# Six K pairs more by Strassen's products in a decoder block: two in the first feed-forward block pair, four in the down projection

## The chip, the cores and the metric

The kernel runs on one core of a Trainium2 chip. The metric is the device time of one execution in microseconds (us), median over three runs. The core's engines are TensorE (PE, matmuls), VectorE (DVE), ScalarE (ACT), GpSimd (POOL) and SyncE (SP, which issues most DMAs). Each works through its own queue of instructions; semaphores order them against each other.

## The reference

One decoder layer on x of 256 x 2048 in float32: an RMSNorm, a mixer block (one wide input projection, four branches, gates, output projection), a second RMSNorm, a SwiGLU feed-forward of width 5632, and a final RMSNorm. The change touches only the feed-forward:

```python
v = rms_norm(h, norm_ffn[l])
h = h + (jax.nn.silu(v @ w_ffn_gate[l]) * (v @ w_ffn_up[l])) @ w_ffn_down[l]
return rms_norm(h, norm_final)
```

## The kernel before

Every large product is made of float32 operands that are split in two: hi is the operand rounded to float32r (by ACT), lo the rest (by DVE), and a product is hi·hi + hi·lo + lo·hi, three matmuls of 128x128 by 128x512 (`mm3s`, lines 215 to 220).

`pair` (line 247) computes the product of the 256 rows with two neighbouring column blocks of 512, wl and wr, over `nkp` K pairs of 2 x 128 rows. Its results are the PSUM tiles q0 and q1 (one for each 128 rows of the output). A K pair is done in one of two ways. The plain one takes 8 products, 24 matmuls, and calls `wpiece` (line 118) for the two weights: a DMA `raw` on SP, `whi` on ACT, `wlo` on DVE; raw, whi and wlo have four buffers each. If the pair's number is in `skps` it is done by the Strassen (Winograd) form with 7 products, 21 matmuls: `s_weights` (line 222) loads the two weights into `sx`, makes four sums on DVE (`se`, `sx`), and splits the two tiles into `sh`/`sl` and `seh`/`sel` (ACT the first of each, DVE the second). sx, sh, sl, seh and sel have two buffers, se one. Four of the products go to PSUM tiles of their own, p1, p5, p6 and p7, which after the last Strassen pair are combined into u. The activations need sums too, `vsh`/`vsl`, for the pairs that are done in this form.

The feed-forward (lines 904 to 921) is 11 calls of `pair`, f = 0 to 10, each with 8 K pairs, gate and up columns as wl and wr. The normalized activations are vth/vtl, transposed by PE from hn: the closures in `later` do this for the last two quarters (12 transposes inside f=0, for pairs 4 to 7), and `run_later` is called at the third pair (`late["at"]` is 2) or, in a call with Strassen pairs that begin earlier, after the last one of them. ACT makes vth, DVE vtl. FS, the pairs whose activation sums are kept, is (0, 2, 3, 5). After each f, `nat_out` (line 318) transposes the hidden block hd and writes it to DRAM as hid (POOL's queue), also through `later`.

The down projection (lines 924 to 972) is two calls of `pair`, cc = 0 and 1, each with 22 K pairs; `h_of` loads hid back into a ring of three slots of `fin` (SP) and splits it into `ah` (ring of four). `split` holds the last pairs back so that q0 finishes first. DSS names the Strassen pairs of either half.

The order of each engine's instructions is made by the scheduler when the kernel is built; it follows the code's order but moves instructions forward where their inputs are ready by its own model.

Of the kernel before, what the change touches and what calls it, by code (L numbers as in the profile page):

```python
# [17 lines left out]
NKT = D // P  # L18
# [11 lines left out]
def hybrid_block_kernel(  # L30
# [13 lines left out]
    w_fg = w_ffn_gate[0]  # L44
    w_fu = w_ffn_up[0]
# [10 lines left out]
    def act(o, i, f=AF.Copy, **kw):  # L56
        return nc.scalar.activation(o, i, f, **kw)  # L57

    def tt(o, a, b, op, eng=None):
        return (eng or nc.vector).tensor_tensor(out=o, in0=a, in1=b, op=op)  # L60
# [9 lines left out]
    late = {"psum": None, "turn": 0, "at": 1}  # L70
# [144 lines left out]
    def mm3s(acc, a, w, first, last, pin=False):  # L215

        for x_, w_, st, sp_ in ((a[0], w[0], first, False), (a[0], w[1], False, False), (a[1], w[0], False, last)):
            m = nc.tensor.matmul(acc, x_, w_, start=st, stop=sp_)  # L218
            if pin:
                tc.keep_in_program_order(m)  # L220

    def s_weights(wl, wr, kp):
        sx, nb = late["sx"], late["sx_bufs"]
        rows = slice(kp * 2 * P, (kp + 1) * 2 * P)
        x_ = sx.tile([P, 4, 512], F32, tag="sx", name="sx", bufs=nb)
        nc.sync.dma_start(x_[:, 0:2, :], wr[rows, :].rearrange("(k p) n -> p k n", p=P))
        nc.sync.dma_start(x_[:, 2:4, :], wl[rows, :].rearrange("(k p) n -> p k n", p=P))
        e = sx.tile([P, 3, 512], F32, tag="se", name="se", bufs=1)
        h, lo = (sx.tile([P, 4, 512], F32R, tag=t, name=t, bufs=nb) for t in ("sh", "sl"))
        eh, el = (sx.tile([P, 3, 512], F32R, tag=t, name=t, bufs=nb) for t in ("seh", "sel"))  # L230
        tt(e[:, 0, :], x_[:, 0, :], x_[:, 1, :], ALU.add)
        tt(x_[:, 0, :], x_[:, 0, :], x_[:, 2, :], ALU.add)
        tt(e[:, 1, :], x_[:, 0, :], x_[:, 1, :], ALU.add)
        tt(e[:, 2, :], e[:, 1, :], x_[:, 3, :], ALU.add)
        act(h, x_)
        tt(lo, x_, rd(h), ALU.subtract)
        act(eh, e)
        tt(el, e, rd(eh), ALU.subtract)
        t1, r2, l1, l2 = ((h[:, i, :], lo[:, i, :]) for i in range(4))
        t3, t2, t4 = ((eh[:, i, :], el[:, i, :]) for i in range(3))  # L240
        return l1, l2, r2, t1, t2, t3, t4

    def run_later():
        while later:
            later.pop(0)()

    def pair(wl, wr, nkp, skps, a_of, upool=None, split=0, quiet=False, at_mid=None, order=None, own=False):

        pq = late["psum"]
        qt = [late["acc"].tile([P, 2, 512], F32, tag=f"q{t}", name=f"q{t}") for t in range(2)]
        q = [[qt[t][:, i, :] for i in range(2)] for t in range(2)]
        p = {}
        ns = len(skps)
        left = {(0, 0): 2 * nkp - ns, (0, 1): 2 * nkp - ns, (1, 0): 2 * nkp - ns, (1, 1): 2 * (nkp - ns),
                1: ns, 5: ns, 6: ns, 7: ns}
        begun = set()
        u = None
        if own:  # L260
            left[1, 0], left[1, 1] = left[1, 0] - 2 * split, left[1, 1] - 2 * split
            left[2, 0] = left[2, 1] = 2 * split
            q = q + [[None, None]]

        def go(i, a, w, pin=False):
            left[i] -= 1
            if i in (1, 5, 6, 7) and i not in begun:
                p[i] = pq.tile([P, 512], F32, tag=f"p{i}", name=f"p{i}")
            if i in ((2, 0), (2, 1)) and i not in begun:
                q[2][i[1]] = pq.tile([P, 512], F32, tag=f"p{(1, 5)[i[1]]}", name="last")  # L270
            mm3s(q[i[0]][i[1]] if isinstance(i, tuple) else p[i], a, w, i not in begun, left[i] == 0, pin)
            begun.add(i)

        held = []
        for n_kp, kp in enumerate(order or range(nkp)):
            if n_kp == late["at"] and (not skps or min(skps) > n_kp) and not quiet:
                run_later()
            blk, sums = a_of(kp, kp in skps)
            if kp in skps:
                l1, l2, r2, t1, t2, t3, t4 = s_weights(wl, wr, kp)  # L280
                go(1, blk(0, 0), l1)
                go(5, sums(0), t1)
                go(7, sums(2), t3)
                go(6, sums(1), t2)
                go((0, 0), blk(1, 0), l2)
                go((0, 1), sums(3), r2)
                go((1, 0), blk(1, 1), t4)
                if kp == max(skps):

                    u = upool.tile([P, 4, 512], F32, tag="u", name="u", bufs=1)  # L290
                    act(u[:, 0, :], p[1])
                    tt(u[:, 1, :], u[:, 0, :], p[6], ALU.add)
                    tt(u[:, 2, :], u[:, 1, :], p[7], ALU.add)
                    tt(u[:, 1:4:2, :], p[5].unsqueeze(1).to_broadcast([P, 2, 512]), u[:, 1:3, :], ALU.subtract)
                    if at_mid is not None:
                        at_mid(u)
                    run_later()
                continue
            rows = slice(kp * 2 * P, (kp + 1) * 2 * P)
            ws = [wpiece(w[rows, :], 2, 512) for w in (wl, wr)]  # L300
            todo = [((t, i), [(blk(j, t), (ws[i][0][:, j, :], ws[i][1][:, j, :])) for j in range(2)])
                    for t in range(2) for i in range(2)]
            if kp >= nkp - split:
                held.append(todo)
                continue
            for i, prods in todo:
                for a, w in prods:
                    go(i, a, w)
        for n in range(4):
            for todo in held:  # L310
                i, prods = todo[n]
                if own and i[0] == 1:
                    i = (2, i[1])
                for a, w in prods:
                    go(i, a, w, pin=True)
        return (qt + [q[2]] if own else qt), u
# [72 lines left out]
    for kt in range(NKT):  # L389
# [11 lines left out]
        if kt % 4 in (1, 2):  # L401
            junk = ap_.tile([P, 512], F32, tag="junk", name="junk")
            q, t = kt // 4, kt % 4 - 1
# [408 lines left out]
    for n, cc in ((2, 0), (0, 0), (1, 1), (3, 1), (2, 1), (0, 1)):  # L812
# [4 lines left out]
        q, gate = pair(w_in[:, col:col + 512], w_in[:, col + 512:col + 1024], NKT // 2, GS, u_of, mp,  # L817
                       split=1)
# [26 lines left out]
    fp = ctx.enter_context(tc.tile_pool(name="fp", bufs=1))  # L845
    FS = (0, 2, 3, 5)
# [35 lines left out]
    for cc in range(2):  # L882
        cs = slice(cc * 1024, (cc + 1) * 1024)
        nc.sync.dma_start(hn[:, :, cs], x[:, cs].rearrange("(t p) n -> p t n", p=P))
        q, _ = pair(w_out[:, cc * 1024:cc * 1024 + 512], w_out[:, cc * 1024 + 512:(cc + 1) * 1024], NKT // 2, (),
                    m_of if cc else m_split, split=1)
# [18 lines left out]
    v_of = a_tiles(vth, vtl, FS, vsh, vsl)  # L905
    for f in range(DFF // 512):
        fs = slice(f * 512, (f + 1) * 512)
        q, u = pair(w_fg[:, fs], w_fu[:, fs], NKT // 2, () if f == 0 else FS if f % 2 else (0, 3, 5), v_of, fp, split=1)
        hd = fp.tile([P, 2, 512], F32, tag="hd", name="hd")

        if u is None:
            for t in range(2):
                act(hd[:, t, :], q[t][:, 0, :], AF.Silu, scale=rstd2[:, t:t + 1])
                tt(hd[:, t, :], hd[:, t, :], q[t][:, 1, :], ALU.mult)
        else:
            for t in range(2):
                o = u[:, 2 * t:2 * t + 2, :]
                tt(o, o, q[t], ALU.add)
                act(u[:, 2 * t, :], u[:, 2 * t, :], AF.Silu, scale=rstd2[:, t:t + 1])
            tt(hd, u[:, 0:4:2, :], u[:, 1:4:2, :], ALU.mult)  # L920
        later.append(lambda hd=hd, f=f: nat_out(hd, hid, f"hid{f}_"))
# [7 lines left out]
    nc.gpsimd.dma_start(gfin, norm_final.partition_broadcast(P))  # L929
    ss3 = small.tile([P, 2, 3], F32, name="ss3", bufs=1)  # L930
    ah = uv.tile([P, 4, 2, 2 * S], F32R, tag="tl", name="ah")
    DSS = ((3, 6, 9, 12), (0, 4, 7, 10, 13))

    def h_of(cc, kp, with_sums):
        if cc == 0 and kp < 4:
# [10 lines left out]
        if with_sums:  # L946
            i = (DSS[cc].index(kp) + 2) % len(FS)
            s_sums(v.rearrange("p (a b) -> p a b", a=2), vsh[:, i], vsl[:, i],
# [7 lines left out]
    for cc in range(2):  # L956
        cs = slice(cc * 1024, (cc + 1) * 1024)
        def at_mid(u):
            for t in range(2):
                o = hn[:, t, cs].rearrange("p (a b) -> p a b", a=2)  # L960
                stt(o, u[:, 2 * t:2 * t + 2, :], rstd2[:, t:t + 1], o, ALU.mult, ALU.add)

        q, u = pair(w_fd[:, cc * 1024:cc * 1024 + 512], w_fd[:, cc * 1024 + 512:(cc + 1) * 1024], NFT // 2, DSS[cc],
                    lambda kp, ws: h_of(cc, kp, ws), fp, split=2 if cc else 1, at_mid=at_mid, own=cc == 1)
# [65 lines left out]
```

## Time and profile before

| | us |
|---|---|
| median of 3 runs (lowest, highest) | 1509.77 (1509.42, 1510.0) |
| profiled execution | 1510.63 |
| its span | 1508.4 |
| PE busy | 1489.2 (99%) |
| DVE busy | 1202.4 (80%) |
| ACT busy | 821.2 (54%) |

The span is the profiled stretch, 2.2 us shorter than the execution's own time. Busy shares are means over stages: f=0 begins at 796.06 us, the down projection at 1262.43, its second half near 1381. Matmuls are pipelined: a matmul's row shows 0.39 us or more, while the next starts 0.23 us after it.

### The profile page before, as it was taken

To read this page: it belongs to the slowest core of one execution; us is meant where nothing else is said; L and a number is where in the kernel's file an instruction comes from. 1 tells how busy PE (TensorE), PEld (TensorE's weight loads), DVE (VectorE), ACT (ScalarE), POOL (GpSimd) and SP (SyncE) were. 2 spreads that over 40 slices of the span, in tenths; PEclk is the share of its full clock that TensorE was granted. 3 is DMA by queue.
4 is the path that set the end of the run, shared out by engine and by line. 5 is a ranking of instruction groups with operands and counts; after the bars stand their busy time and mean duration, and the time that the engine had idled before them with its cause. 6 is when DMAs were issued, how large, how long until landed. Compare 5 with 4: busy or idle time off the path is not lost.

```text
span 1508.4 us, 18519 instructions
## 1 busy us (share of the span) xinstructions
PE 1489.2 (99%) x6763; PEld 1225.8 (81%) x6763; DVE 1202.4 (80%) x1400; ACT 821.2 (54%) x944; POOL 71.7 (5%) x94
## 2 busy tenths in 40 slices
PE   8999999999999999999999999999999999999997
PEld 7778888888788888887888888888888888888885
DVE  4756755678898889887568899999989899897865
ACT  5544844555554555544456555555555555655643
POOL 3000300001000000000000000000000000001000
PEclk9999999999999999999999999999999999999999
DMA  7645455556666676656557666576657568786663
GB/s 239 211 150 160 133 187 163 160 187 226 209 210 198 220 261 199 209 191 209 186 180 251 218 216 220 197 237 201 234 179 237 189 223 279 254 279 223 205 213 115
DMA packets 158603, 311.54 MB, mean 207 GB/s; under 512 B 10608, under 2 KB 12720, under 8 KB 158384
## 3 DMA queue, kind: packets, MB, share of 16 engines
q1 hardware_dynamic: 154528, 297.87, 60.4%
q0 software_dynamic: 3952, 12.49, 2.4%
q8 instruction: 53, 0.87, 0.2%
q14 instruction: 38, 0.31, 0.1%
q10 hardware_dynamic: 32, 0.01, 0.0%
HBM read 301.41 MB, written 8.91 MB: 206 GB/s over the span
## 4 chain that ended last, share of the span: by engine, by line
PE 96%; DVE 1%; DMA 1%; issue 1%; ACT 0%; SPq 0%; POOLq 0%; POOL 0%; ACTq 0%; DVEq 0%
PE q L218 61%; PE acc L133 20%; PE p L218 11%; PE ps L165 2%; DMA xq<-in_x_dram 0%; DVE wlo L60 0%; DMA raw<-in_w_in_dram 0%; PE ps L541 0%; PE ps L737 0%; PE ps L560 0%; PE ps L499 0%; ACT whi L57 0%; PE ps L607 0%; PE ps L754 0%; PE ps L693 0%
## 5 line engine op out<-in xcount | busy, mean ns | idle before, releaser
L60 DVE TENSOR_TENSOR wlo<-raw,whi 128x1024 fp32r<-128x1024 f32 (+1 forms) x412 | 504.3, 1230 | 188.7 <-ACT whi L57 186.0
L57 ACT ACTIVATE whi<-raw 128x1024 fp32r<-128x1024 f32 (+1 forms) x412 | 431.7, 1050 | 393.4 <-PE q L218 166.0
L57 ACT ACTIVATE sh<-sx 128x2048 fp32r<-128x2048 f32 x62 | 118.8, 1916 | 116.6 <-PE q L218 41.8
L133 PE MATMUL acc<-wlo,uth 128*128 128x512 f32 (+1 forms) x448 | 173.9, 391 | 0.0
L133 PE MATMUL acc<-whi,utl 128*128 128x512 f32 (+1 forms) x448 | 173.8, 389 | 0.0
L60 DVE TENSOR_TENSOR sl<-sx,sh 128x2048 fp32r<-128x2048 f32 x62 | 141.9, 2289 | 36.1 <-ACT sh L57 36.0
L133 PE MATMUL acc<-whi,uth 128*128 128x512 f32 (+1 forms) x448 | 167.6, 390 | 0.6 <-DVE nat L64 0.4
L218 PE MATMUL q<-wlo,vth 128*128 128x512 f32 x424 | 165.8, 391 | 0.0
L218 PE MATMUL q<-whi,vtl 128*128 128x512 f32 x424 | 165.6, 391 | 0.0
L218 PE MATMUL q<-whi,vth 128*128 128x512 f32 x424 | 164.5, 391 | 0.0
L218 PE MATMUL q<-whi,ah 128*128 128x512 f32 x512 | 159.5, 389 | 0.0
L218 PEld LDWEIGHTS q<-whi,ah 128*128 128x128 f32 x512 | 96.1, 188 | 19.9
L60 DVE TENSOR_TENSOR sel<-se,seh 128x1536 fp32r<-128x1536 f32 x62 | 108.6, 1751 | 4.5 <-ACT seh L57 4.1
L57 ACT ACTIVATE seh<-se 128x1536 fp32r<-128x1536 f32 x62 | 91.7, 1479 | 22.3 <-PE q L218 20.3
L218 PE MATMUL q<-wlo,ah 128*128 128x512 f32 x256 | 99.8, 390 | 0.3 <-DVE wlo L60 0.3
L133 PEld LDWEIGHTS acc<-wlo,uth 128*128 128x128 f32 x448 | 84.8, 189 | 16.9 <-issue 1.0
L133 PEld LDWEIGHTS acc<-whi,utl 128*128 128x128 f32 x448 | 84.8, 189 | 16.5 <-issue 0.7
L133 PEld LDWEIGHTS acc<-whi,uth 128*128 128x128 f32 x448 | 81.7, 188 | 16.9 <-issue 0.7
L218 PE MATMUL q<-wlo,uth 128*128 128x512 f32 x240 | 93.8, 391 | 0.0
L218 PE MATMUL q<-whi,uth 128*128 128x512 f32 x240 | 93.8, 391 | 0.0
L218 PE MATMUL q<-whi,utl 128*128 128x512 f32 x240 | 93.5, 389 | 0.0
L60 DVE TENSOR_TENSOR se<-sx 128x512 f32<-128x512 f32 x124 | 86.2, 695 | 8.8 <-DMA sx<-in_w_in_dram 7.4
(393 smaller groups left out, 2535.6 us busy)
## 6 DMA issues: line engine op xcount, KB each, us to landing
raw<-in_w_in_dram SPq DMA_DIRECT2D x156, 512.0 KB, 3.4
raw<-in_w_ffn_down_dram SPq DMA_DIRECT2D x70, 512.0 KB, 5.1
raw<-in_w_ffn_gate_dram SPq DMA_DIRECT2D x53, 512.0 KB, 4.1
raw<-in_w_ffn_up_dram SPq DMA_DIRECT2D x53, 512.0 KB, 4.8
sx<-in_w_in_dram SPq DMA_DIRECT2D x36, 512.0 KB, 4.3
sx<-in_w_ffn_up_dram SPq DMA_DIRECT2D x35, 512.0 KB, 3.7
sx<-in_w_ffn_gate_dram SPq DMA_DIRECT2D x35, 512.0 KB, 4.7
raw<-in_w_branch_dram SPq DMA_DIRECT2D x32, 512.0 KB, 4.4
```

The lines of the kernel that those rows point to most:

```text
L57: return nc.scalar.activation(o, i, f, **kw)
L60: return (eng or nc.vector).tensor_tensor(out=o, in0=a, in1=b, op=op)
L133: m = nc.tensor.matmul(acc, x_, w_, start=st, stop=sp_)
L165: m = nc.tensor.transpose(pt[:, i * S + t * P:i * S + (t + 1) * P], nat[:, t, (c0 + i) * P:(c0 + i + 1) * P], ident)
L218: m = nc.tensor.matmul(acc, x_, w_, start=st, stop=sp_)
```

## The change

Three numbers and one condition. f=0 gets two Strassen pairs, 0 and 3, and works through its pairs in the order 1, 2, 4, 0, 5, 3, 6, 7. DSS goes from 4 to 5 pairs in the first half and from 5 to 8 in the second. The condition for `run_later` asks whether the first Strassen pair has come in the order so far, instead of whether its number is below.

```diff
-            if n_kp == late["at"] and (not skps or min(skps) > n_kp) and not quiet:
+            if n_kp == late["at"] and (not skps or skps[0] not in (order or range(nkp))[:n_kp + 1]) and not quiet:
                 run_later()
...
-        q, u = pair(w_fg[:, fs], w_fu[:, fs], NKT // 2, () if f == 0 else FS if f % 2 else (0, 3, 5), v_of, fp, split=1)
+        q, u = pair(w_fg[:, fs], w_fu[:, fs], NKT // 2, (0, 3) if f == 0 else FS if f % 2 else (0, 3, 5), v_of, fp,
+                    split=1, order=(1, 2, 4, 0, 5, 3, 6, 7) if f == 0 else None)
...
-    DSS = ((3, 6, 9, 12), (0, 4, 7, 10, 13))
+    DSS = ((2, 5, 8, 11, 14), (0, 2, 5, 7, 10, 12, 15, 17))
```

The built program has 6650 matmul instructions instead of 6668. In the first down half the first Strassen pair is now 2, which is in the first three of the order, so the closures of the last hidden block run after pair 14 instead of at the third pair.

The order on PE in f=0, behind the 12 transposes. whi_6618 and whi_6624 are the two weights of pair 4 after; sh_6656, sl_6657, seh_6658 are those of pair 0. After:

```order
L165 MATMUL ps_6607<-ident_73,hn_5764 128x128 x3
L218 MATMUL q0_6497<-whi_6618,vth_5777 128x512
L218 MATMUL q0_6497<-wlo_6619,vth_5777 128x512
L218 MATMUL q1_6498<-whi_6618,vth_5777 128x512
L218 MATMUL q1_6498<-wlo_6619,vth_5777 128x512
L218 MATMUL q0_6497<-whi_6618,vtl_5778 128x512
...
L218 MATMUL q1_6498<-wlo_6625,vth_5777 128x512
L218 MATMUL q1_6498<-whi_6624,vtl_5778 128x512
L218 MATMUL p1_6668<-sh_6656,vth_5777 128x512
L218 MATMUL p5_6672<-sh_6656,vsh_5768 128x512
L218 MATMUL q0_6497<-sh_6656,vth_5777 128x512
L218 MATMUL p7_6676<-seh_6658,vsh_5768 128x512
```

Before:

```order
L165 MATMUL ps_6607<-ident_73,hn_5764 128x128 x3
L218 MATMUL q0_6497<-whi_6618,vth_5777 128x512
L218 MATMUL q0_6497<-wlo_6619,vth_5777 128x512
L218 MATMUL q0_6497<-whi_6618,vtl_5778 128x512
L218 MATMUL q0_6497<-whi_6618,vth_5777 128x512
L218 MATMUL q0_6497<-wlo_6619,vth_5777 128x512
```

Before, whi_6618 was a weight of pair 2, whose vth and vtl were there long ago; after, it is one of pair 4, whose vth and vtl come out of these transposes, and the Strassen pair 0 stands directly behind.

The order on ACT at the same place, behind the last vth. After:

```order
L57 ACTIVATE vth_5777<-ps_6607,prm_523 128x256
L57 ACTIVATE vsh_5768<-s_temp_6585 128x512
L57 ACTIVATE whi_6773<-raw_6771 128x1024
L57 ACTIVATE whi_6779<-raw_6777 128x1024
L57 ACTIVATE sh_6656<-sx_6652 128x2048
L57 ACTIVATE seh_6658<-se_6655 128x1536
```

Before:

```order
L57 ACTIVATE vth_5777<-ps_6607,prm_523 128x256
L57 ACTIVATE whi_6690<-raw_6688 128x1024
L57 ACTIVATE vsh_5768<-s_temp_6585 128x512
L57 ACTIVATE whi_6696<-raw_6694 128x1024
L57 ACTIVATE whi_6726<-raw_6724 128x1024
```

Two whi of a later plain pair stand ahead of sh_6656; whi_6773 lies in the buffer of whi_6618, whi_6779 in that of whi_6624.

The order on SP near the end of the first down half; hid10_0 and hid10_1 are the two halves of the last hidden block, read by pairs 20 and 21; raw_10907 and raw_10913 are the weights of pair 19 after, raw_10810, raw_10816, raw_10849 and raw_10855 those of pairs 17 and 18 before. After:

```order
L120 DMA raw_10907<-in_w_ffn_down_dram 128x2x512
L940 DMA fin_10099<-hid0_1_7094 128x512
L940 DMA fin_10099<-hid10_1_10746 128x512
L120 DMA raw_10913<-in_w_ffn_down_dram 128x2x512
L940 DMA fin_10099<-hid10_0_10738 128x512
L120 DMA raw_10946<-in_w_ffn_down_dram 128x2x512
```

Before:

```order
L120 DMA raw_10810<-in_w_ffn_down_dram 128x2x512
L939 DMA fin_10087<-hid10_0_10175 128x512
L120 DMA raw_10816<-in_w_ffn_down_dram 128x2x512
L120 DMA raw_10849<-in_w_ffn_down_dram 128x2x512
L939 DMA fin_10087<-hid10_1_10183 128x512
L120 DMA raw_10855<-in_w_ffn_down_dram 128x2x512
```

The loads of the last hidden block have moved from among the weights of pairs 17 and 18 to those of pair 19, and hid10_1 stands ahead of hid10_0 and between the two weights of pair 19.

## Rows read from the trace of the kernel before

**Rows 1.** The page, parts 1 and 4: busy us and share; chain by engine.

```profile
PE 1489.2 (99%) x6763; PEld 1225.8 (81%) x6763; DVE 1202.4 (80%) x1400; ACT 821.2 (54%) x944; POOL 71.7 (5%) x94
PE 96%; DVE 1%; DMA 1%; issue 1%; ACT 0%; SPq 0%; POOLq 0%; POOL 0%; ACTq 0%; DVEq 0%
```

**Rows 2.** Timeline of PE: start, duration, line, operation; four matmuls, first and last.

```profile
1203.30 0.39 PE L218 MATMUL p<-sh,vth 128*128 128x512 f32 x1
...
1203.98 0.39 PE L218 MATMUL p<-sh,vsh 128*128 128x512 f32 x1
```

**Rows 3.** Windows: length, busy us of PE, PEld, DVE, ACT, POOL, clock, DMA.

```profile
796.10:885.00 88.90, 88.90 (x406) 73.75 (x405) 76.50 (x85) 55.08 (x58) 1.93 (x3) 1.00 0.69 228
1420.60:1436.24 15.64, 15.64 (x71) 12.96 (x70) 13.05 (x17) 9.63 (x10) 0.00 (x0) 1.00 0.50 160
```

**Rows 4.** Timeline of PE at the transposes inside f=0.

```profile
807.23 0.40 PE L218 MATMUL q<-whi,vtl 128*128 128x512 f32 x1
807.47 1.47 PE L165 MATMUL ps<-ident,hn 128*128 128x128 f32 x12
808.69 0.48 PE L218 MATMUL q<-whi,vth 128*128 128x512 f32 x1
```

**Rows 5.** Timeline of ACT behind these transposes.

```profile
809.04 0.46 ACT L57 ACTIVATE vth<-ps,prm 128x256 fp32r<-128x256 f32 x1
...
810.11 2.96 ACT L57 ACTIVATE vth<-ps,prm 128x256 fp32r<-128x256 f32 x7
```

**Rows 6.** Timeline of DVE behind them.

```profile
810.31 0.47 DVE L68 SCALAR_TENSOR_TENSOR vtl<-ps,prm,vth 128x256 fp32r<-128x256 f32 x1
...
812.09 1.26 DVE L68 SCALAR_TENSOR_TENSOR vtl<-ps,prm,vth 128x256 fp32r<-128x256 f32 x3
```

**Rows 7.** Groups of DVE in 870 to 1257: busy us, mean ns, idle before.

```profile
L60 DVE TENSOR_TENSOR wlo<-raw,whi 128x1024 fp32r<-128x1024 f32 x82 | 98.8, 1218 | 6.8 <-ACT whi L57 6.8
L60 DVE TENSOR_TENSOR sl<-sx,sh 128x2048 fp32r<-128x2048 f32 x33 | 75.6, 2290 | 17.3 <-ACT sh L57 17.3
L60 DVE TENSOR_TENSOR sel<-se,seh 128x1536 fp32r<-128x1536 f32 x32 | 56.0, 1751 | 1.0 <-ACT seh L57 0.8
L60 DVE TENSOR_TENSOR se<-sx 128x512 f32<-128x512 f32 x65 | 44.5, 685 | 0.7
```

**Rows 8.** Timeline of ACT in the down projection: seh and sh.

```profile
1287.04 1.47 ACT L57 ACTIVATE seh<-se 128x1536 fp32r<-128x1536 f32 x1
1288.41 1.90 ACT L57 ACTIVATE sh<-sx 128x2048 fp32r<-128x2048 f32 x1
```

**Rows 9.** Timeline of PE: start of the down projection, transposes of hid10, a wait.

```profile
1262.10 0.39 PE L218 MATMUL q<-whi,vtl 128*128 128x512 f32 x1
1262.43 0.47 PE L218 MATMUL q<-whi,vsh 128*128 128x512 f32 x1
...
1274.57 1.04 PE L165 MATMUL ps<-ident,hd 128*128 128x128 f32 x8
...
1342.10 0.84 PE L218 MATMUL q<-whi,ah 128*128 128x512 f32 x3
1343.22 0.50 PE L218 MATMUL q<-wlo,ah 128*128 128x512 f32 x1 [0.28 <-DVE wlo L60]
```

**Rows 10.** Timeline of POOL: the writes of hid10 are issued.

```profile
1276.95 1.39 POOL L325 DMA_DIRECT2D hid<-hd  x2 [13.83 <-ACT hd L57]
```

**Rows 11.** Line 325, the writes of hid: issue to landing.

```profile
DMA to landing us min/median/max: 2.5/4.6/8.4
```

**Rows 12.** Line 120, the loads of raw, in 1300 to 1345: issue to landing.

```profile
DMA to landing us min/median/max: 4.5/5.3/6.4
```

**Rows 13.** Windows for the clock: columns as in rows 3.

```profile
8.00:16.00 8.00, 6.52 (x32) 5.65 (x33) 4.16 (x6) 4.00 (x9) 5.58 (x10) 0.79 1.07 361
702.00:704.00 2.00, 1.07 (x5) 0.92 (x6) 2.00 (x5) 0.87 (x1) 0.00 (x0) 1.00 1.25 222
```

**Rows 14.** Timeline of PE: a matmul behind a wait, earlier in the kernel.

```profile
702.93 0.47 PE L218 MATMUL q<-whi,mh 128*128 128x512 f32 x1 [1.21 <-ACT whi L57]
```

## The prediction, on record before the change was timed

> **What bounds the kernel now.** I read the page's busy line first and then its chain of waits: TensorE (PE) is busy 99% of the span and 96% of the chain that ended last is PE [rows 1]. So time falls only if PE gets less to do, and rises wherever PE has to wait for something it did not wait for before. The change takes work from PE and gives it to VectorE (DVE), so DVE is the second thing to read. It is 80% busy over the span [rows 1], but the windows by stage differ: 76.50 of 88.90 us in the first two feed-forward blocks (f=0 and f=1, 796.10 to 885.00), and 13.05 of 15.64 us in one period of the down projection's second half [rows 3]. There is room, but little, and whether a result is late is decided by the place of each instruction in its queue. Last I read three places event by event: the transposes inside f=0 [rows 4 to 6], the end of the feed-forward part and the end of the first down half [rows 9].
>
> **What the change takes from PE.** A plain K pair is 24 matmuls, a Strassen pair is 7 products of 3, so 21. Six pairs fewer of the plain kind: 18 matmuls less. Four matmuls in a row start 1203.30 to 1203.98, 0.227 us apart [rows 2], so 18 x 0.227 = 4.1 us. PE is the chain in both parts, so all 4.1 us count: 1.36 in f=0, 0.68 in the first down half, 2.04 in the second.
>
> **What it adds to DVE and ScalarE (ACT).** A plain pair costs DVE two wlo, 2 x 1.22 us; a Strassen pair four adds of 0.69, one sl of 2.29 and one sel of 1.75, about 6.5 by their durations [rows 7]. In the down projection sums of the activations come on top (four small adds and a vsl; some 1.5 us). ACT trades two whi of 1.06 for one sh of 1.92 and one seh of 1.48 [rows 8], 1.3 us more. For f=0 that is 2 x 4.1 = 8.2 us more DVE; the spare in 796.10 to 885.00 is 12.4 [rows 3], so on the average it fits. In the second down half five pairs in 22 become eight. A period of two Strassen and three plain pairs is 114 matmuls, 25.9 us of PE; from the period of one and two (69 matmuls, DVE 13.05) I get for DVE, with a plain down pair at 2 x 1.22 plus one 0.68 split, about 3.1, and a Strassen one at 13.05 - 6.2 = 6.9 by this window: 2 x 6.9 + 3 x 3.1 = 23. Summed from single durations instead, a Strassen down pair is up to 8.3 and the period 25.3, 98% of PE's. Either way DVE stays under PE, and two buffers of each Strassen tile let it run a pair ahead. I take no wait there; the upper bound is a rival below.
>
> **f=0, first wait: the transposes.** Before, 12 transposes stand at 807.47 and matmuls of older data (whi, vth of earlier pairs) follow from 808.69 without a gap [rows 4]. After, all 48 matmuls of pairs 1 and 2 stand ahead of the transposes or are spent, and the first matmuls behind them are those of pair 4, which read the vth and vtl that these same transposes have to yield (first piece of order shown with the change). PE's place of the transposes and the order of ACT and DVE up to there are the same in both programs, so before's times hold. The first vth is the one at 809.04, ready at 809.50 [rows 5]; PE wants it at 808.69: 0.86 us with a 0.05 us signal. Four matmuls later it wants the first vtl, 810.31 + 0.47 [rows 6]: 0.38. Two later the second vth of pair 4, the fourth of the seven from 810.11 (811.18 to 811.69): 0.45. Four later its vtl, the second of the three from 812.09 (812.49 to 812.96): 0.37. Sum 2.06, and 14 more matmuls (3.18) bring PE to 816.20.
>
> **f=0, second wait: the Strassen pair 0 directly behind.** It wants sh_6656 at 816.20. In ACT's order (second piece) two plain whi stand ahead of it. The buffer of the second, whi_6779, is that of whi_6624, last read by the 14th of those matmuls, 815.97 + 0.39 = 816.36. So whi_6779 runs from 816.42, with 0.97 until the next can start, and sh from 817.39 for 1.91 [rows 8]: 819.35, a wait of 3.15. Three matmuls on, PE wants seh_6658 at 820.03. DVE does wlo, se, wlo, se ahead of it, the second wlo only behind whi_6779: 817.90, 819.05, then se to 819.73, seh 1.47 to 821.32: 1.29. sl is ready at 822.0 when wanted. Sum of f=0: 2.06 + 3.15 + 1.29 = 6.5 us. The bounds: 2.06 alone if the whi's buffer were free sooner and sh early (only the transposes' wait is then left), and 9.5 if each of pair 0's two waits is longer by one wlo of 1.22 that slips ahead on DVE and pair 3 is late by the same. I take 6.5. After it DVE runs without a pause through pairs 3, 6 and 7, but PE, itself late by 6.5, gives it that much more room; I put nothing there.
>
> On the queue: ACT's rows start in the program's order, the vth of 809.04 before the seven of 810.11 [rows 5]. The Trainium skill, "PSUM — Partial Sum Buffer", section "Engine vs sequencer instructions", says that the queues of ScalarE, VectorE and GpSimd are strict FIFO. By that rule sh cannot pass the blocked whi_6779 and the 3.15 stands; could it pass, it would start at 816.2, behind DVE's second add, and the wait would be about 1.9 and the sum 1.2 us less.
>
> **The two ends of the first down half.** At its start PE now waits for DVE to take q0 out of the last feed-forward block: before this cost 0.10 (1262.10 to 1262.43 is 0.33 instead of 0.227 [rows 9]). DVE's order there now has the new pair 2's add and another wlo near it; followed with the durations of [rows 7], q0 is free 0.6 late: +0.5 (bounds 0 and 1.9, one wlo and one add). At its end the transposes of the last hid move from the third pair to the last Strassen pair, 14, since the changed condition no longer lets them run early. SP's queue (third piece) now holds raw_10913, weight of pair 19, behind the load of hid10_1, which waits for its write. From the first of these transposes to the first matmul with that weight PE has 69 matmuls of 0.227 and 8 transposes, 1.04 together [rows 9]: 16.7 us. The chain meanwhile is 2.4 from transposes to issue (1274.57 to 1276.95 before [rows 9, 10]), landing of hid 4.6, at most 8.4 [rows 11], landing of raw 5.3, at most 6.4 [rows 12], and whi 1.06: 13.4 at the medians, 18.3 at worst, 1.6 late. I take 0.5, between. The wait of before ahead of 1343.22, which the row puts at 0.28 for a wlo [rows 9] and which against the pitch is 0.44 (three matmuls from 1342.10 should end their turn at 1342.78), goes, since its pairs change: -0.4.
>
> **The sum.** -4.1 + 6.5 + 0.5 + 0.5 - 0.4 = +3.0 us. The profiled execution took 1510.63 (span 1508.4 and 2.2 around it), so 1513.6 on its scale; the median of the runs is 0.86 less, so 1512.8. One per thousand either way cannot be told: I count within 0.2%, 3.0 us, as no change (1506.75 to 1512.79), which lies just at my sum.
>
> **Rivals.**
> A (forecast): waits of f=0 as worked out, 1511 to 1515. Chance 0.55.
> B: the waits are partly covered, as whi_6779 or the adds come sooner than I follow them; f=0 costs 2 to 4, the rest nothing: -4.1 + 3 = -1, about 1509 (1508 to 1511). For it: DVE has 12.4 us spare in the stretch. Against: the buffer of whi_6779 is freed by PE itself. 0.2.
> C, the other side: PE loses nothing anywhere, since every new product is ready: 1509.8 - 4.1 = 1505.7. It is decided by sh_6656: were it ready by 816.2, and pair 4 not in want of its transposes. Against it stands the order of PE, where pair 4 follows them. 0.07.
> D: DVE becomes the bound in the second down half, at 8.3 a Strassen pair: with the signals between queues counted it would exceed PE's 25.9 by 1 to 1.5 in each of three periods: +4 on A, 1516 to 1518. For it: DVE at 98%. Against: 13.05 of 15.64 in the window. 0.12.
> E: the clock of PE falls in f=0 as its 4.4 us of waits around pair 0 leave it idle. At the kernel's start the granted clock is 0.79 over 8:16 [rows 13], a mean of the levels 1.2 and 2.4 GHz, so about 8 x 0.21 = 1.7 us lost; A + 1.7 is 1514.5. Against it: a wait of 1.21 for a whi ahead of 702.93 [rows 14] left 1.00 in 702:704 [rows 13]. The chance is 0.06. The Trainium skill, "TensorE: Matmul & The Clock Gate", section "HAM oscillation — how this bites in real kernels", tells of bursts of matmuls that start cold after each wait for data; by that rule E would come, while our row of a shorter wait speaks against it, and none of this length lies in this part.
>
> **How the numbers follow.** The forecast is A's 1512.8. Range 1508.3 to 1516.6: it takes in A, B and E and the lower part of D, and leaves out C and D's end; the bounds of f=0 alone (2.1 to 9.5) would give 1508.4 to 1515.8. Faster by over 0.2%: C and a piece of B, 0.09. Slower by over 0.2%: half of A and a little more, since what I left at nothing can only add, D and E: 0.51. Within: 0.40.
>
> **What would show it.** In the profile after: PE idle before the first q<-whi,vth behind the 12 transposes of f=0, and 3 us before p<-sh directly behind that pair's 24 matmuls, released by ACT sh, then over 1 us released by ACT seh; ACT's whi idle until PE's q. Later blocks and the second down half without PE waits, PE's busy time less by about 4. Wrong: if p<-sh follows without a gap (B or C), if idle stretches before sl or sel repeat in the second down half (D), or the granted clock near 820 lies under 1 (E).

## The result: 6.5 us slower, and the profile after

The changed kernel takes 1516.31 us (median of 5 runs, 1515.90 to 1519.98), before 1509.77 (5 runs, 1508.56 to 1511.46): 6.5 us more, or 1.0043 by the two medians. The record's ratio of the runs is 1.0051, with a 95% interval of 1.0039 to 1.0062; the ratios and intervals below are of that kind. Slower was forecast, but by 3.0 us; the profiled executions are 1516.06 and 1510.63, 5.4 apart.

The page of the changed kernel, parts 1 and 4, answers to [rows 1]:

```profile
PE 1488.6 (98%) x6745; PEld 1223.8 (81%) x6745; DVE 1236.6 (82%) x1448; ACT 830.7 (55%) x949; POOL 76.7 (5%) x94
PE 94%; DVE 2%; DMA 1%; issue 1%; ACT 1%; SPq 0%; POOLq 0%; POOL 0%; ACTq 0%; DVEq 0%
```

PE has 18 matmuls fewer, but its busy time falls by 0.6 only, and the chain has 2% of DVE and 1% of ACT in it instead of 1% and 0%. To see where, I cut the execution at three matmuls that both kernels have: the first of f=0, the first of the down projection, the last of all. Until the first of f=0 the code is the same. The starts are read off PE's timeline.

| us | before | after |
|---|---|---|
| start to f=0 | 796.06 | 796.52 |
| f=0 to the down projection | 466.37 | 475.13 |
| down projection to its last matmul | 234.63 | 231.31 |
| last matmul to the end | 11.34 | 11.27 |

So the down projection gave more than its 12 matmuls (2.72) and the feed-forward part lost 8.76. The timeline of PE in the changed kernel, f=0, answers to [rows 4]; the figure in brackets is idle time and what ended it:

```profile
807.93 1.47 PE L165 MATMUL ps<-ident,hn 128*128 128x128 f32 x12
810.37 0.50 PE L218 MATMUL q<-whi,vth 128*128 128x512 f32 x1 [0.98 <-ACT vth L57]
...
811.66 0.73 PE L218 MATMUL q<-whi,vtl 128*128 128x512 f32 x2
812.56 0.49 PE L218 MATMUL q<-whi,vth 128*128 128x512 f32 x1 [0.16 <-ACT vth L57]
...
813.84 0.49 PE L218 MATMUL q<-whi,vtl 128*128 128x512 f32 x1
...
816.93 0.39 PE L218 MATMUL q<-whi,vtl 128*128 128x512 f32 x1
820.36 0.76 PE L218 MATMUL p<-sh,vth 128*128 128x512 f32 x1 [3.04 <-issue]
820.92 0.63 PE L218 MATMUL p<-sh,vsh 128*128 128x512 f32 x1
821.35 0.63 PE L218 MATMUL q<-sh,vth 128*128 128x512 f32 x1
822.26 1.22 PE L218 MATMUL p<-seh,vsh 128*128 128x512 f32 x2 [0.28 <-ACT seh L57]
823.28 0.63 PE L218 MATMUL q<-seh,vth 128*128 128x512 f32 x1
...
826.27 0.54 PE L218 MATMUL q<-sh,vsh 128*128 128x512 f32 x1
826.65 0.39 PE L218 MATMUL q<-sl,vsh 128*128 128x512 f32 x1
```

Read starts, not lengths: what a start lies beyond the one before it by more than 0.227 is lost. Behind the transposes there are four waits, 1.22, 0.26, 0.33 and 0.25, for vth and vtl of pair 4 (for the first, 807.93 to 810.37 less the 1.22 that the 12 transposes took before); ahead of p<-sh 3.20 (816.93 to 820.36). Then, from 820.36 to 826.27, most matmuls start 0.43 apart instead of 0.23, and ahead of p<-seh there is a wait of 0.68. The windows of the changed kernel (columns as in [rows 3]) say why; the clock is the third number from the end:

```profile
816.00:818.00 2.00, 1.32 (x6) 0.75 (x4) 1.97 (x3) 1.66 (x2) 0.00 (x0) 1.00 0.00 0
818.00:820.00 2.00, 0.00 (x0) 0.00 (x0) 2.00 (x3) 2.00 (x2) 0.00 (x0) 0.94 0.24 40
820.00:822.00 2.00, 1.62 (x3) 0.83 (x3) 2.00 (x3) 1.54 (x2) 0.00 (x0) 0.50 0.85 259
824.00:826.00 2.00, 2.00 (x6) 1.52 (x6) 1.93 (x3) 0.00 (x0) 0.00 (x0) 0.50 0.93 296
826.65:830.00 3.35, 3.35 (x16) 2.78 (x15) 2.79 (x3) 2.69 (x2) 0.00 (x0) 1.00 0.14 54
```

The clock fell to the lower level (1.2 GHz) while PE idled (0.94 in 818 to 820, where PE did nothing), and was back at 1.00 by 826.65. The bracket "issue" at 820.36 names no cause: ACT's timeline has it.

```profile
816.03 1.06 ACT L57 ACTIVATE whi<-raw 128x1024 fp32r<-128x1024 f32 x1 [1.00 <-PE q L218]
817.40 1.06 ACT L57 ACTIVATE whi<-raw 128x1024 fp32r<-128x1024 f32 x1 [0.31 <-PE q L218]
818.37 1.89 ACT L57 ACTIVATE sh<-sx 128x2048 fp32r<-128x2048 f32 x1
820.72 1.48 ACT L57 ACTIVATE seh<-se 128x1536 fp32r<-128x1536 f32 x1 [0.46 <-DVE se L60]
```

sh ends at 820.26, and PE starts 0.1 later. sh follows on two whi that waited for PE to let go of their buffers, and seh waits for DVE, whose timeline up to there is full:

```profile
816.52 0.69 DVE L60 TENSOR_TENSOR sx<-sx 128x512 f32<-128x512 f32 x1
817.13 1.22 DVE L60 TENSOR_TENSOR wlo<-raw,whi 128x1024 fp32r<-128x1024 f32 x1
818.27 0.68 DVE L60 TENSOR_TENSOR se<-sx 128x512 f32<-128x512 f32 x1
818.87 1.22 DVE L60 TENSOR_TENSOR wlo<-raw,whi 128x1024 fp32r<-128x1024 f32 x1
820.01 0.68 DVE L60 TENSOR_TENSOR se<-se,sx 128x512 f32<-128x512 f32 x1
```

In the down projection PE waits once, at its start, for q0 (answers to [rows 9]: 1.14 between two starts instead of 0.33; the add that it waits for yields u). A wait for hid10 and the one of [rows 9] at 1343.22 are not there, and with DVE at 103.62 of 116.00 us the second half runs without a gap:

```profile
1270.51 0.39 PE L218 MATMUL q<-whi,vtl 128*128 128x512 f32 x1
1271.65 0.47 PE L218 MATMUL q<-whi,vsh 128*128 128x512 f32 x1 [0.75 <-DVE u L60]
```

```profile
1387.00:1503.00 116.00, 116.00 (x514) 96.01 (x512) 103.62 (x127) 64.79 (x76) 11.81 (x4) 1.00 0.56 185
```

### The profile page after: what moved, and what is told of

It reads as the page before. It is cut to its first block, busy times and chain, and to the rows that moved or that the text cites. A ratio compares the mean times of both kernels' runs of the same rounds, so it can differ in the third digit from the quotient of the medians.

```text
span 1514.2 us, 18539 instructions
## 1 busy us (share of the span) xinstructions
PE 1488.6 (98%) x6745; PEld 1223.8 (81%) x6745; DVE 1236.6 (82%) x1448; ACT 830.7 (55%) x949; POOL 76.7 (5%) x94
## 4 chain that ended last, share of the span: by engine, by line
PE 94%; DVE 2%; DMA 1%; issue 1%; ACT 1%; SPq 0%; POOLq 0%; POOL 0%; ACTq 0%; DVEq 0%
PE q L218 58%; PE acc L133 20%; PE p L218 12%; PE ps L165 2%; DVE wlo L60 1%; DMA raw<-in_w_ffn_up_dram 1%; DMA xq<-in_x_dram 1%; ACT whi L57 0%; DMA raw<-in_w_in_dram 0%; PE ps L541 0%; PE ps L737 0%; PE ps L560 0%; PE ps L499 0%; DVE u L60 0%; PE ps L607 0%
## 5 line engine op out<-in xcount | busy, mean ns | idle before, releaser
L57 ACT ACTIVATE whi<-raw 128x1024 fp32r<-128x1024 f32 (+1 forms) x400 | 418.8, 1049 | 375.1 <-PE q L218 172.9
L60 DVE TENSOR_TENSOR wlo<-raw,whi 128x1024 fp32r<-128x1024 f32 (+1 forms) x400 | 488.0, 1226 | 166.7 <-ACT whi L57 163.7
L57 ACT ACTIVATE sh<-sx 128x2048 fp32r<-128x2048 f32 x68 | 130.2, 1914 | 103.7 <-DVE sx L60 54.0
L60 DVE TENSOR_TENSOR sl<-sx,sh 128x2048 fp32r<-128x2048 f32 x68 | 157.2, 2312 | 23.7 <-ACT sh L57 23.5
L218 PE MATMUL q<-whi,ah 128*128 128x512 f32 x448 | 140.5, 389 | 0.0
L60 DVE TENSOR_TENSOR sel<-se,seh 128x1536 fp32r<-128x1536 f32 x68 | 119.1, 1751 | 8.8 <-ACT seh L57 8.7
L57 ACT ACTIVATE seh<-se 128x1536 fp32r<-128x1536 f32 x68 | 100.5, 1478 | 44.0 <-DVE se L60 27.7
L60 DVE TENSOR_TENSOR se<-sx 128x512 f32<-128x512 f32 x136 | 94.4, 694 | 8.1 <-DMA sx<-in_w_in_dram 6.1
L218 PEld LDWEIGHTS q<-whi,ah 128*128 128x128 f32 x448 | 84.0, 188 | 17.4
L218 PEld LDWEIGHTS q<-whi,vth 128*128 128x128 f32 x408 | 76.6, 188 | 17.2 <-ACT vth L57 1.8
```

## The experiments

The same code up to f=0 took from 795.0 to 800.2 us in the 14 profiled executions of this study, which puts some us of spread on every profiled time. Beside each median I therefore give the stages of the profiled execution: f=0 to the down projection (466.37 before), then to the last matmul (234.63 before). Where a time of before stands beside a median, it is that of the runs on the same chip.

**f=0 alone.**

```diff
-    DSS = ((2, 5, 8, 11, 14), (0, 2, 5, 7, 10, 12, 15, 17))
+    DSS = ((3, 6, 9, 12), (0, 4, 7, 10, 13))
```

> The changed f=0 (two Strassen pairs, new order) with the old Strassen pairs of the down projection. Theory (all of the loss is made in f=0: waits of 5.6 to 6 us and 2.5 us of half clock behind them, less 1.4 us of matmuls saved): about 1517.7, that is 8 us above before, with the PE wait of about 3 us before p<-sh and a granted clock of 0.5 behind it. Rival (DVE, busier in the down projection, makes the loss): within 2 us of before. Rival (the clock falls because of something later than f=0): no stretch of 0.5 near 822.

1518.78 against 1509.87, ratio 1.0058 (1.0045 to 1.0071); stages 475.47 and 234.01. The wait of 3.20 for sh and the 0.43 pitch are the changed kernel's. f=0 alone makes the whole loss. The down projection, whose code is that of before, took 0.6 less than before, without the wait of 0.44: that wait was not a matter of the Strassen pairs there.

**The down projection alone.**

```diff
-        q, u = pair(..., (0, 3) if f == 0 else FS if f % 2 else (0, 3, 5), ..., order=(1, 2, 4, 0, 5, 3, 6, 7) if f == 0 else None)
+        q, u = pair(..., () if f == 0 else FS if f % 2 else (0, 3, 5), ..., order=None)
```

> The old f=0 (no Strassen pair) with the new Strassen pairs of the down projection. Theory: 12 matmuls fewer (2.7 us), the 0.44 us wait of before gone, a wait of 0.8 for q0 at the start of the down projection: about 1507.3, 2.4 below before. Rival (DVE as the bound of the second down half): 1510 or more. No stretch of a clock under 1.00 in either theory.

1508.89 against 1509.87, ratio 0.9994 (0.9985 to 1.0003), so not told apart by medians; stages 466.37 and 232.47, 2.2 below before. The 2.7 of the matmuls are there, but a new wait of 0.68 for a wlo at 1356.54 (some 60 matmuls behind the last Strassen pair of the first half) takes a part back, and the expected wait of 0.8 for q0 did not come.

**PE's idle time filled.**

```diff
+                if order and kp == 0:
+                    d = bank()
+                    for _ in range(14):
+                        tc.keep_in_program_order(nc.tensor.matmul(d, vth[:, 0, :P], vth[:, 0:2, :], start=True, stop=True))
                 l1, l2, r2, t1, t2, t3, t4 = s_weights(wl, wr, kp)
```

> The changed kernel with 14 matmuls whose result nothing reads put on PE directly ahead of the first product of Strassen pair 0 in f=0, where PE idles for 3.2 us. They read only activations that are long there. Theory (the half clock behind the wait comes from the idle time itself): the wait is filled, p<-sh starts as before at about 820.4, the clock stays at 1.00 and the kernel is 2 to 2.5 us faster than the changed one, about 1514, though it has 14 matmuls more. Rival (the slow matmuls of 820 to 826 come from the new tiles or from DMA and DVE traffic, not from idling): the same pitch of 0.43 there and 1516.3 to 1519.5.

The timeline of PE and the windows in this kernel:

```profile
817.98 3.33 PE L283 MATMUL ps<-vth 128*128 128x512 f32 x14
821.19 0.47 PE L218 MATMUL p<-sh,vth 128*128 128x512 f32 x1
821.50 0.39 PE L218 MATMUL q<-sh,vth 128*128 128x512 f32 x1
821.73 0.40 PE L218 MATMUL p<-sh,vsh 128*128 128x512 f32 x1
823.10 0.74 PE L218 MATMUL p<-seh,vsh 128*128 128x512 f32 x2 [0.97 <-ACT seh L57]
...
866.18 0.50 PE L218 MATMUL p<-sh,vth 128*128 128x512 f32 x1 [2.66 <-ACT sh L57]
```

```profile
822.00:826.00 4.00, 3.03 (x14) 2.34 (x14) 3.97 (x3) 1.04 (x1) 0.00 (x0) 1.00 0.72 198
866.10:869.10 3.00, 2.52 (x9) 1.46 (x10) 2.94 (x2) 1.41 (x2) 0.00 (x0) 1.00 0.03 10
```

The clock stays at 1.00 and the pitch at 0.23: the half clock came from idling, not from the tiles or the traffic. The wait for seh, at full clock, is 1.14. From the first matmul of f=0 to q<-sh,vsl of pair 0 it is 28.47 us here (797.27 to 825.74) and 30.35 in the changed kernel (796.52 to 826.87), so the clock's net price is 1.9. The median is not better, 1519.21 (ratio 1.0062, 1.0050 to 1.0074; stages 476.02 and 231.22): with the 14 matmuls in the program the scheduler put the instructions behind them, on PE, ACT and DVE, in another order, and a wait of 2.82 came up in f=1, at 866.18. That part of the expectation missed. That long wait left the clock at 1.00.

**sh let past the two whi.**

```diff
-            ws = [wpiece(w[rows, :], 2, 512) for w in (wl, wr)]
+            ws = [wpiece(w[rows, :], 2, 512, pin=bool(order) and kp == 6) for w in (wl, wr)]
```

> The changed kernel, but whi and wlo of pair 6 in f=0 are held behind the sums of pair 3, so that ACT's sh_6656 no longer stands behind them. Theory: sh starts when its sums are made, 817.3 instead of 818.4, so the wait of 3.2 becomes about 2.1 and that for seh about 0.7 instead of 1.3. If a wait of 2.1 leaves the clock at 1.00: about 1516.3 - 1.1 - 2.8 = 1512.4. If the clock falls as well: about 1514.7. Rival (the queue order is not the cause, sh waits for its data): unchanged, 1516.3.

ACT and PE in this kernel:

```profile
815.92 1.91 ACT L57 ACTIVATE sh<-sx 128x2048 fp32r<-128x2048 f32 x1 [2.21 <-DVE sx L60]
```

```profile
817.93 0.47 PE L218 MATMUL p<-sh,vth 128*128 128x512 f32 x1 [1.97 <-issue]
...
838.53 0.50 PE L218 MATMUL p<-sh,vth 128*128 128x512 f32 x1 [2.93 <-ACT sh L57]
```

```profile
817.90:822.00 4.10, 3.77 (x10) 2.67 (x11) 4.07 (x3) 1.31 (x1) 0.00 (x0) 0.59 0.18 17
```

The wait at pair 0 is 2.13, as expected for an sh that waits for its data only; the clock fell behind it all the same. But the held whi then stand late, and the first Strassen pair of f=1 waits 3.09 at 838.53, with a half clock again: 1519.67 (ratio 1.0070, 1.0058 to 1.0082), stages 479.04 and 231.33. The queue order was the cause of 1.1 us of the wait, and putting it right by hand only moved the loss; the 1512.4 to 1514.7 expected for that missed.

**The transposes one pair earlier.**

```diff
+    late["at"] = 1
     for f in range(DFF // 512):
```

> The changed kernel, but in f=0 the closures (the 12 transposes) run at the second pair instead of the third, so that 17 matmuls of pair 2 stand between the transposes and pair 4; in the first down half the hid10 transposes run at the second pair too. Theory (the transposes' wait is for vth and vtl of pair 4): the four waits of 2.0 us behind the transposes go; the wait for sh stays near 3.2, as whi_6779 still waits for the end of pair 4, and that for seh too. If the clock falls behind one long wait by itself: 0.5 again, f=0 to the down projection 475.1 - 2.4 = 472.7 us, about 1514. If it falls only where more idle time comes together (the run before had 2.82 us by itself at a clock of 1.00, and 2.13 behind four short waits at 0.59): 1.00, 470.8 us, about 1512. Rival (the transposes themselves are late): the waits stay, 475.

The edit also moves hid10's transposes to the second pair of the first down half. The four waits behind the 12 transposes are gone. The wait for sh grew to 3.85 (812.93 to 817.01) instead of staying at 3.2. DVE and ACT in this kernel:

```profile
813.14 1.22 DVE L60 TENSOR_TENSOR wlo<-raw,whi 128x1024 fp32r<-128x1024 f32 x1 [0.55 <-ACT whi L57]
814.28 0.68 DVE L60 TENSOR_TENSOR sx<-sx 128x512 f32<-128x512 f32 x1
```

```profile
815.00 1.91 ACT L57 ACTIVATE sh<-sx 128x2048 fp32r<-128x2048 f32 x1 [0.54 <-DMA raw<-in_w_ffn_up_dram]
```

```profile
817.00:824.80 7.80, 6.73 (x17) 5.00 (x18) 7.14 (x8) 3.50 (x3) 0.00 (x0) 0.56 0.69 222
```

A wlo that waits for its whi (812.05 to 813.11, behind 2.15 of idle ACT) stands ahead of the add sx on DVE, and sh waits for that add: it ends at 814.96 and sh starts at 815.00, whatever the bracket names. The whi itself starts just behind the end of PE's 18th matmul of pair 4 (811.96), the last that reads that pair's first weight, whose buffer it takes in the changed kernel. The clock fell behind this wait without short ones ahead, while PE waited another 1.23 for seh (817.55 to 819.00). 1513.54 against 1510.08, ratio 1.0027 (1.0018 to 1.0036); stages 473.87, 1.3 less than the changed kernel, and 231.31.

**The held whi and the earlier transposes together.**

> Both edits of the two kernels before: transposes at the second pair, and whi and wlo of pair 6 held behind the sums of pair 3. Theory: sh waits only for DVE's adds, which come earlier by the earlier transposes: waits at pair 0 of 0.6 and 0.7; but pair 6, whose whi come behind seh of pair 3, is late by about 3 us as when held before (3.09 there). f=0 to the down projection 469 to 471 us, clock at 1.00 at pair 0. If holding pair 6 costs nothing here: 466.4. The median 1507 to 1511.

1516.86 against 1510.08, ratio 1.0046 (1.0034 to 1.0058); stages 473.78 and 233.06. At pair 0 a wait of 2.20 that left the clock at 1.00; at 837.14 one of 2.10, and 0.56 behind it; in the second down half one of 1.62 that the changed kernel does not have. Waits of 0.6 and 0.7 were expected at pair 0, and 469 to 471 for the stage: the expectation missed.

**Pair 0 behind pair 5.**

```diff
-split=1, order=(1, 2, 4, 0, 5, 3, 6, 7) if f == 0 else None)
+split=1, order=(1, 2, 4, 5, 0, 3, 6, 7) if f == 0 else None)
...
+    late["at"] = 1
     for f in range(DFF // 512):
```

> The changed kernel with the order 1, 2, 4, 5, 0, 3, 6, 7 in f=0 and the closures run at the second pair: 24 more matmuls of pair 5 stand ahead of Strassen pair 0. Theory (the loss is only the time between PE's place of pair 0 and its sums): no wait behind the transposes, none or under 0.5 for sh and seh, clock 1.00; f=0 to the down projection 466.4 - 1.4 + 0 to 0.9 (wait for q0) = 465.0 to 465.9, the rest 231.3 + 11.3; the median 1505.5 to 1507, 3 to 4 below before. Rival (DVE in f=0 is full, the waits only move to pair 3 or to f=1): 468 to 472, the median 1509 to 1513.

The rival was right on the stage (468 to 472). PE in this kernel, pair 0 and then pair 3:

```profile
821.42 0.73 PE L218 MATMUL p<-seh,vsh 128*128 128x512 f32 x2 [0.54 <-ACT seh L57]
828.34 0.50 PE L218 MATMUL p<-sh,vth 128*128 128x512 f32 x1 [2.54 <-ACT sh L57]
```

```profile
828.30:833.50 5.20, 4.75 (x13) 3.53 (x14) 5.11 (x4) 1.96 (x2) 0.00 (x0) 0.67 0.33 91
```

Pair 0 is nearly in time (0.70), pair 3 is late by 2.70, with the clock down behind it. DVE is busy 9.38 of the 10 us from 820 to 830. 1515.14, above the rival's 1513, ratio 1.0031 (1.0020 to 1.0042); stages 471.98 and 231.33, the first the least of all with two Strassen pairs in f=0, and still 5.6 above before.

**Pair 6 between the two.** The same with the order 1, 2, 4, 5, 0, 6, 3, 7.

> As the kernel with order 1, 2, 4, 5, 0, 3, 6, 7, but with pair 6 between the two Strassen pairs: 1, 2, 4, 5, 0, 6, 3, 7. Theory: the same saving, 465.0 to 465.9 for f=0 to the down projection, if DVE has the sums of pair 3 in time in either place; if two Strassen pairs in a row are too much for DVE (6.5 us each against 4.8 of PE), this one is faster by up to 1.7 us. Rival: pair 3, now last but one, makes the combination of p1, p5, p6, p7 late and f=1 waits: 467 or more.

1517.91, ratio 1.0052 (1.0041 to 1.0064); stages 474.72 and 231.32. In f=0 there is 0.70 at 820.54; the other waits moved into f=1: 0.92 at 841.76, 1.75 at 853.41 and 1.53 at 855.73, the clock at 0.60 behind the last. This is the rival's side.

**One Strassen pair in f=0, at two places.** The down projection is the changed one, its hid10 transposes at the second pair.

```diff
-(0, 3) if f == 0 else ... order=(1, 2, 4, 0, 5, 3, 6, 7) if f == 0 else None
+(5,) if f == 0 else ... order=(0, 1, 2, 3, 4, 6, 5, 7) if f == 0 else None
...
+    late["at"] = 1
     for cc in range(2):
```

> The down projection as in the kernel with early hid10 transposes, and one Strassen pair in f=0, pair 5, as the last but one: order 0, 1, 2, 3, 4, 6, 5, 7. The transposes stand in front of pair 2 as in the kernel before. Theory (DVE cannot make the sums of two Strassen pairs in f=0 beside the transposes' vtl, but those of one that comes late): no wait of PE in f=0, clock 1.00, 3 matmuls fewer: 465.7 us to the down projection, in all 3.5 below before. Rival (f=1 pays, since its pair 0 follows too soon): a wait of 1 to 3 us near 860, 467 to 469.

1516.43 against 1510.57, ratio 1.0035 (1.0022 to 1.0048); stages 469.87 and 235.12. f=0 has no wait, as the theory said, but f=1 has 0.51 at 848.13, in its first pair, and 2.17 at 862.65 (the rival), with the clock at 1.00; in the first down half a wlo makes PE wait 2.01, and there the clock falls:

```profile
862.60:866.00 3.40, 2.94 (x10) 1.83 (x11) 3.37 (x2) 1.38 (x1) 0.00 (x0) 1.00 0.16 40
1362.60:1367.10 4.50, 4.44 (x12) 3.50 (x13) 4.50 (x6) 0.00 (x0) 0.00 (x0) 0.62 0.87 280
```

With (3,) and the order 0, 1, 2, 4, 5, 3, 6, 7:

> The same with pair 3 as the Strassen pair of f=0 at the sixth place: order 0, 1, 2, 4, 5, 3, 6, 7. Theory: 465.7 us to the down projection too. But here two whi of pair 4 follow directly on the transposes as in the changed kernel: if the order of PE puts pair 4 ahead of the rest of pair 2, the four short waits of 2 us come back, 467.7; the order shows pair 2 behind the transposes, so I expect none.

1514.31, ratio 1.0033 (1.0021 to 1.0044); stages 471.03 and 234.55; 2.82 in f=1, at 858.77, with the clock at 0.63, and no waits behind the transposes; 1.37 and 1.56 in the down projection. The 465.7 expected missed in both. One pair is already too many for f=0 and the start of f=1, whose pairs 0, 2, 3 and 5 follow.

**The down projection alone, hid10 early.** The second kernel of this section with `late["at"] = 1` ahead of the loop over cc.

> The old f=0, the new Strassen pairs of the down projection, and the hid10 transposes of the first down half at its second pair, as in the kernel before, instead of behind pair 14. Theory: f=0 to the down projection 466.4 us as before; the wait of 0.68 for a wlo that the same down projection had with the late transposes goes, as DVE and ACT have less to do near pair 15: 231.3 to 232 from there to the last matmul, in all 3 us below before, median about 1507. Rival (that wait has nothing to do with the transposes): 232.5, 2.1 below before.

1512.22 against 1510.57, ratio 1.0011 (0.9998 to 1.0024); stages 466.37 and 233.89. The wait of 0.68 became 1.55 (1354.95) and one of 0.52 was added (1390.55): the late place of the transposes was not its cause, and the theory missed.

**The second half alone.**

```diff
-    DSS = ((2, 5, 8, 11, 14), (0, 2, 5, 7, 10, 12, 15, 17))
+    DSS = ((3, 6, 9, 12), (0, 2, 5, 7, 10, 12, 15, 17))
```

> The old f=0 and the old first down half; only the second down half has its eight Strassen pairs instead of five. Theory: 9 matmuls fewer, 2.04 us, nothing else: 234.6 - 2.0 = 232.6 us from the start of the down projection to the last matmul, with the wait of 0.44 near 1343 still there, median about 1507.7. Rival (DVE is the bound of the second half): waits of 1 us or more between 1381 and 1497, 234 or more.

1508.74 against 1510.57, ratio 0.9990 (0.9981 to 0.9999); stages 466.37 and 232.00, and no step of PE beyond its pitch by more than 0.12 from f=0 to the last matmul. That is 2.6 below before: 2.0 for the 9 matmuls, and 0.6 that f=0 alone, with the old down projection, gave as well; the wait of 0.44 was expected to stay and went. This version is faster than both kernels, than the one before by a per mille, with an interval that just leaves out 1. DVE has 101.19 of the 116 us there:

```profile
1381.00:1497.00 116.00, 113.28 (x500) 93.47 (x498) 101.19 (x124) 67.43 (x80) 7.23 (x4) 1.00 0.56 182
```

## Why the prediction was wrong

Each step by its own numbers, all from the profiled executions:

| step | forecast | measured |
|---|---|---|
| 18 matmuls fewer | -4.1 | -4.1 |
| waits behind the transposes | 2.06 | 2.06 |
| wait for sh | 3.15 | 3.20 |
| from p<-sh to the return of the clock | 1.29 | 3.3 |
| first matmul behind a wait, other steps | 0 | 0.7 |
| wait for q0 | +0.5 | +0.8 |
| hid10's load | +0.5 | 0 |
| the old wait of 0.44, and the rest of the down projection | -0.4 | -0.6 |
| sum | +3.0 | +5.4 |

Rows two to five make f=0's term: 6.5 forecast, 9.3 measured (8.76, plus 1.36 of matmuls saved, less the 0.81 that q0 cost more than before). The mechanism of A came out place by place, with sh behind two held whi and seh behind DVE's queue. The step that failed is the one against rival E: from a whi's wait of 1.21 ahead of 702.93, a third as long, behind which the clock had stayed at 1.00, I took the clock's fall for unlikely, gave it 0.06, and left its cost out of the sum. It came: 0.50 in 820 to 822 and in 824 to 826. Half clock and seh's wait overlap: PE's slow matmuls used up a part of the wait (0.68 instead of the 1.14 of the kernel with the filled wait), so of the 3.3 us behind p<-sh some 1.9 are the clock's by that kernel. That is near the 1.7 that E put on it, in part by luck: E took its price from the clock at the kernel's start, where nothing overlapped it.

A second, smaller miss is a term at nothing: the matmul behind each wait starts its successor 0.33 later instead of 0.227 (810.37 to 810.71), 0.11 four times behind the transposes; the other 0.3 of that row are many small steps.

The 2.06 behind the transposes was hit in its sum only, also by luck. The first of the four waits is 0.36 longer than worked out (1.22 against 0.86), and each of the other three 0.12 shorter, as PE came to them 0.11 later than its pitch says. The first vth stands on ACT behind a whi that waits for the landing of its raw, and the raw came later. ACT's row of this whi, before and after:

```profile
808.08 1.06 ACT L57 ACTIVATE whi<-raw 128x1024 fp32r<-128x1024 f32 x1 [0.72 <-DMA raw<-in_w_ffn_up_dram]
808.90 1.06 ACT L57 ACTIVATE whi<-raw 128x1024 fp32r<-128x1024 f32 x1 [1.08 <-DMA raw<-in_w_ffn_up_dram]
```

So the times of before did not hold up to there, as the prediction took them to. In the other kernels with the waits at this place the first was 0.77 to 1.31.

The two stages together lost 5.4; the medians differ by 6.5. The 1.1 between them lies within the spread of the same code ahead of f=0 (795.0 to 800.2), but which part of the kernel made it in those runs was not seen.

The other steps: the second down half kept PE fed, so D was wrong, as expected, with DVE at 89% of it (103.62 of 116.00). The prediction's 98% there goes with 8.0 us a Strassen pair; with its 8.3 the period's 25.3 would be 25.9, all of PE's. PE did not wait for hid10's load, as the medians of its landing had it (13.4 of 16.7 us). What moved these transposes behind pair 14 is the new first Strassen pair, 2: the old condition would have held them back too, and the new one acts in f=0 alone, where the old one would have held the 12 transposes until both Strassen pairs were through. The old wait of 0.44 went, but not because its pairs changed: it was gone with the old pairs too. The upper bound of f=0, 9.5, would by its own words be 6.5 and three times 1.22, 10.2; the measured 9.3 lies under either.

And one sentence of the working did not hold beyond this kernel: that the spare of DVE in the first two blocks (12.4 of 88.9 us) leaves room for two Strassen pairs "on the average". Moving the pairs about found no place: with pair 0 later, pair 3 waited; with pair 3 later, f=1; with a single pair, f=1 again. The windows of before show where the spare lay:

```profile
796.10:809.00 12.90, 12.90 (x66) 10.82 (x65) 8.01 (x12) 7.08 (x9) 0.72 (x1) 1.00 0.92 319
809.00:841.00 32.00, 32.00 (x143) 26.48 (x142) 30.64 (x37) 22.53 (x27) 0.00 (x0) 1.00 0.70 232
```

DVE has 4.9 us to spare to the end of the transposes, but 1.4 in the 32 us behind them, where by the prediction's figure the changed kernel wants 8.2 more; the rest of the spare lies behind 841.

What stays open: when the clock falls. From f=0 on these kernels have twelve waits of 2 us or more; behind nine of them the clock fell (2.01, 2.10, 2.13, 2.70, 2.82, 3.09, 3.20 twice, 3.85), behind three it did not (2.17, 2.20, 2.82). A wait of 2.82 did both, so length alone does not decide it.

## What to carry to other kernels

Work taken from a full engine and given to a partly idle one pays where the second engine's idle time lies, so read its share by the stage and by what its queue can start there, not over the span. A wait of 2 us or more on PE can cost more than itself: behind nine of twelve here the clock fell, so count a half clock behind it as likely, not as a rival of 0.06. Test the parts of a change one by one: here three pairs of six (the second down half's) were worth having, and two cost more than all six gave.

## What the runs showed of the hardware that was not expected

A stretch at half clock lasted from shortly before 820 (0.94 in 818 to 820) to about 826.6 in the changed kernel, and took most of 817.0 to 824.8 (0.56) behind the wait of 3.85, though PE worked without long pauses in most of it. PE's start-up part, the same code in every kernel, took 795.0 to 800.2 us in 14 profiled executions, more than any effect of this change but the loss in f=0. A part of that spread is the clock again: in the three kernels where f=0 began last (at 797.27 with the filled wait, 799.75 with f=0 alone, 800.20 with pair 5) PE idled 1.6 to 1.8 us near 50 us, and the clock fell there too (0.50 in 49.60 to 53.00 of the first); in the other eleven PE idled at most 1.0 us there, and it did not.
